# Laying out the bias tables behind the fourth residual tile

## The chip, the cores and the metric

The kernel runs on one core of a Trainium2 chip. The metric is the device time of one execution in microseconds (us), as the median of several runs. One execution was also profiled; every trace number comes from it.

The names of the profile: PE is the matrix engine (PEld its weight loads), DVE the vector engine, ACT the scalar engine, POOL the general engine, SP the engine that here does nothing but issue DMA transfers. All engines run their own instruction streams in order and wait for each other through semaphores.

## The reference

Two layers over 1024 latent tokens of width 1024 and 256 context tokens. Layer zero is grouped attention (16 query heads, 4 key heads, rotary positions), layer one is neighbourhood attention with a learned relative-position bias. Cut to what matters:

```python
for i in range(2):
    hx = rms_norm(x, norm_g[i]) * (1 + sc_x) + sh_x          # adaLN; the same for ctx
    hc = rms_norm(ctx, norm_g[i]) * (1 + sc_c) + sh_c
    if i == 0:
        yx, yc = gqa_axial_mixer(hx, hc, ...)                # (softmax attention * silu(z)) @ a_w_out
    else:
        yx, yc = neighbourhood_mixer(hx, hc, ..., b_rpb)     # scores + bias from b_rpb (16 x 15 x 31)
    x = x + g_x * yx
    if i == 0:
        ctx = ctx + g_c * yc
return rms_norm(x, final_norm_g)
```

In the second layer a query at row r and column c sees 8 rows by 16 columns of keys, and its score gets `rpb[head, dr, dc]`.

The change's title counts from one: "layer one's output projection" is that of the first of the two, called layer zero here.

## The kernel before

Tokens are tiled by 128: eight tiles of x (0 to 7) and two of the context (8 and 9). Weights and activations are split into a high and a low float16 part, and each product is three matmuls. The stages in order of time:

- 0 to about 95 us: modulation columns, the norm of x, keys and values of layer zero. Here the keys are normalised, rotated and split (helper `norm_rope_split`, lines 735 to 762), and their high half is copied to the upper partitions by a DMA (`k<-k`, L831).
- to about 690 us: layer zero's attention, head pair by head pair (`a_proj`, `a_att`, `q_att`). For each pair the row maxima are gathered (`rows`): one DMA transposes them (`zt<-zmax`, L1002), and further DMAs lay the rows into the query tile (`q<-zt`, L1006 and L1008); the score matmuls `st` (L1183, L1184) read that tile. Halves of a last row of heads are taken from `oa` and `oar`, and their outputs for the context from `oc`.
- about 627 to 766 us: layer zero's output projection (`a_out`, matmuls `poa`, L1275). For each token tile t the residual rows are loaded into a tile `x1{t}` (L1262; the trace calls it `x<-in_x`), the gated projection is added, and the sum is written to `x1_d` in DRAM (L1282, `x_d<-x`). The `x1` tiles share one ring of four buffers, so x10 to x13 are loaded first and x14 follows when x10 is free. x13 is the fourth residual tile. The tiles live in a pool that opens when the query projection's pool is closed.
- to about 790 us: the norm of layer one's input (`b_ln`, with DMA transposes `hb_hi<-h16b` and `hb_lo<-l16b`, L661), then its projections (`pb`, `pvz`).
- to the end: layer one's attention (`b_att`), its output projection (`pob`) and the final norm.

The bias of layer one is laid out in DRAM in two steps, both of DMAs from DRAM to DRAM on SP's queue. Sixteen transfers (L1318) copy, for each of 16 grid rows, runs of 16 floats from the input `rpb` into `toe`. Eight transfers (L1321) copy strips of 384 floats from `toe` into `tabd`. Later sixteen loads (L1332) bring one head's table each to SBUF (`tb<-tabd`), where POOL adds the masks (L1333 to L1335) and DVE adds the table to the scores (L1444).

The order of the work on every engine is not the order in which the program writes it. A class `Planner` takes all instructions, builds their dependencies (`graph`), simulates them with a cost of its own for each, and on each engine always starts, of the instructions that are ready, the one with the smallest key; an engine does not stay idle while one is ready, except that SP holds back while its counted DMA work is more than 2 us ahead (`AHEAD`). In the first pass the key is the place in the program; in five more passes it is, for all engines but PE, a due time found by going back from the planned PE order (`deadlines`), and for PE the start in the pass before. The order with the shortest planned time is kept (`refine`) and tied to the instructions (`apply`). So one added tie can move instructions on all engines.

`BEHIND` is a list of pairs (late, early) of tile names. For each pair `graph` finds the DMA copy that writes the late tile and makes it a successor of the DMA copy that writes the early one. The tie is a soft one: the late transfer may start once the early one has been issued, and need not wait for it to land.

Of the kernel before, what the change touches and what calls it, by code (L numbers as in the profile page):

```python
# [40 lines left out]
PFB, PHB, PTB = 5, 5, 8  # L41


BEHIND = [(f"xstage{t}", "wskv7") for t in range(4, 8)]


class Planner:
# [114 lines left out]
    def graph(self):  # L162
# [14 lines left out]
        for x in self.ins:  # L177
# [9 lines left out]
            i = len(self.node)  # L187
# [43 lines left out]
        writer = {}  # L231
        for i, x in enumerate(self.node):
            if type(x).__name__ == "InstDMACopy" and x.outs and hasattr(x.outs[0], "bass_ap"):
                writer.setdefault(x.outs[0].bass_ap.tensor.name.rsplit("_", 1)[0], i)
        for late, early in BEHIND:
            self.soft.add((writer[early], writer[late]))
            self.pred[writer[late]].add(writer[early])

        self.glued = set()
        first = last = None  # L240
# [1418 lines left out]
```

## Time and profile before

| | |
|---|---|
| median of 3 runs | 1366.02 us (1362.78 to 1366.33) |
| the profiled execution's own time | 1365.58 us |
| its span, first to last instruction | 1363.8 us |
| granted PE clock over the span | 0.999 |
| PE, DVE, ACT, POOL busy | 98%, 74%, 67%, 49% |
| toe issues (16) | 47.5 to 65.1 us |
| tabd issues (8) | 68.0 to 77.9 us |
| x1 loads for x10 to x13 | 634.3 to 638.1 us |
| first table load to SBUF | 784.3 us |

The page of the profile gives busy times of the engines over the span, queues, the chain of work that ended last, and groups of instructions by line. Lines such as "PE st L1184 <- DMA q<-zt" say that PE's instruction of line 1184, writing tile st, waited for a DMA that writes q from zt. The engine name SPq means SP's instruction queue, which issues DMAs. A stage's row gives the stretch, its length, and the busy time of each engine in it with the number of instructions in brackets.

### The profile page before, as it was taken

The numbers are of one execution on the slowest core, as the hardware profiler recorded it, in microseconds if no ns is written. First come the engines' busy times: TensorE is split into PE (matmuls) and PEld (weight loads), VectorE is DVE, ScalarE is ACT, GpSimd is POOL, SyncE is SP. The second block draws the span as 40 slices with busy tenths as digits, with TensorE's granted clock in tenths as the row PEclk, the third lists the DMA queues.
The fourth block names the chain that finished last, engine by engine and source line by source line (L and its number), as shares of the span: only waits on it lengthen the run. The fifth ranks groups of instructions, "written<-read, shape, count | busy, mean of one in ns | idle before, by whom it ended". The sixth has DMA issues, their size and how long they took to land.

```text
span 1363.8 us, 34709 instructions
## 1 busy us (share of the span) xinstructions
PE 1329.9 (98%) x13183; PEld 927.6 (68%) x13183; DVE 1003.1 (74%) x2647; ACT 910.2 (67%) x2186; POOL 664.7 (49%) x855
## 2 busy tenths in 40 slices
PE   9999999999999999999999999999999999999897
PEld 6457777777777777776554486777768686867543
DVE  5788788878788789887276846777776867777743
ACT  3653788888787876878632437777776777786711
POOL 2573787777778775788743201312222222332332
PEclk9999999999999999999999999999999999999999
DMA  9652577878789777847066725666576656677932
GB/s 352 186 162 76 108 145 156 154 161 166 149 152 169 146 150 138 172 145 210 10 171 175 178 80 120 125 132 138 117 153 110 156 96 146 113 159 141 194 101 102
DMA packets 426959, 198.23 MB, mean 145 GB/s; under 512 B 382560, under 2 KB 389664, under 8 KB 426792
## 3 DMA queue, kind: packets, MB, share of 16 engines
q1 hardware_dynamic: 426216, 195.98, 65.3%
q8 instruction: 103, 1.69, 0.5%
q14 instruction: 64, 0.52, 0.1%
q10 hardware_dynamic: 576, 0.03, 0.0%
HBM read 90.51 MB, written 15.22 MB: 78 GB/s over the span
## 4 chain that ended last, share of the span: by engine, by line
PE 68%; DVE 11%; ACT 9%; DMA 5%; POOL 3%; issue 3%; SPq 1%; DVEq 0%; POOLq 0%; ACTq 0%
PE pa L946 11%; PE pb L1360 9%; PE pvz L1393 9%; PE poa L1275 7%; PE pob L1566 6%; PE st L1183 2%; PE st L1184 2%; PE pkv L817 2%; ACT bpf L1464 2%; PE pm L976 2%; PE bpv L1473 1%; PE pv L1052 1%; PE qpv L1104 1%; PE pv L1053 1%; PE pv L1051 1%
## 5 line engine op out<-in xcount | busy, mean ns | idle before, releaser
L1045 POOL TENSOR_TENSOR pl<-pf,ph 128x256 f16<-128x256 f32 x340 | 234.1, 714 | 58.2 <-ACT pf L1170 44.5
L1045 POOL TENSOR_TENSOR bph<-bpf,bph 128x256 f16<-128x256 f32 (+1 forms) x128 | 99.9, 790 | 319.5 <-ACT bpf L1464 256.3
L946 PE MATMUL pa<-wa,x 128*128 128x256 f16 x1536 | 213.4, 272 | 0.1
L1360 PE MATMUL pb<-hb_hi,wb 128*128 128x512 f16 (+1 forms) x640 | 193.3, 358 | 1.4 <-DVE bk L1379 1.0
L1393 PE MATMUL pvz<-wb,hb_hi 128*128 128x256 f16 x1024 | 175.4, 273 | 0.6 <-DVE bk L1379 0.3
L946 PEld LDWEIGHTS <-x 128*128 128x128 f16 x1536 | 143.2, 97 | 35.7 <-issue 1.3
L1168 ACT ACTIVATE ph<-st 128x512 f16<-128x512 f32 x200 | 119.1, 604 | 60.7 <-PE st L1184 50.0
L1360 PEld LDWEIGHTS <-wb 128*128 128x128 f16 x960 | 92.7, 98 | 72.5 <-issue 2.9
L1393 PE MATMUL pvz<-wb,hb_lo 128*128 128x256 f16 x512 | 139.6, 273 | 0.0
L1170 ACT ACTIVATE pf<-st 128x512 f32<-128x512 f32 x200 | 119.3, 609 | 1.7 <-POOL pl L1045 1.6
L977 DVE TENSOR_REDUCE mxp<-pm 128x1 f32<-128x512 f32 x160 | 107.9, 684 | 13.7 <-PE pm L976 12.3
L1045 POOL TENSOR_TENSOR qpp<-qpf,qpp 128x512 f16<-128x512 f32 x84 | 97.9, 1186 | 38.4 <-ACT qpf L1127 32.2
L1360 PE MATMUL pb<-hb_lo,wb 128*128 128x512 f16 (+1 forms) x320 | 114.4, 358 | 0.0
L1393 PEld LDWEIGHTS <-hb_hi 128*128 128x128 f16 x1024 | 97.1, 98 | 24.2 <-DVE bk L1379 1.1
L1051 PE MATMUL pv<-v,ph 128*128 128x65 f16 x800 | 104.0, 193 | 0.2 <-ACT ph L1168 0.2
L1052 PE MATMUL pv<-v,ph 128*128 128x64 f16 x800 | 104.0, 195 | 0.0
L1053 PE MATMUL pv<-v,pl 128*128 128x65 f16 x800 | 101.4, 192 | 0.5 <-POOL pl L1045 0.5
L1566 PE MATMUL pob<-wob,ob 128*128 128x512 f16 x384 | 86.7, 379 | 2.6 <-DVE bmx L1444 0.9
L1051 PEld LDWEIGHTS <-ph 128*128 128x128 f16 x800 | 75.8, 97 | 19.0 <-ACT ph L1168 0.7
L1462 ACT ACTIVATE bph<-bpf,bnx 128x384 f16<-128x384 f32 (+1 forms) x128 | 68.7, 582 | 27.2 <-DVE bnx L1454 27.1
L1052 PEld LDWEIGHTS <-ph 128*128 128x128 f16 x800 | 75.5, 97 | 12.6
L1053 PEld LDWEIGHTS <-pl 128*128 128x128 f16 x800 | 76.1, 99 | 10.5 <-POOL pl L1045 1.6
(272 smaller groups left out, 3812.1 us busy)
## 6 DMA issues: line engine op xcount, KB each, us to landing
wg<-in_w_mod SPq DMA_DIRECT2D x64, 256.0 KB
wsb<-in_b_in SPq DMA_DIRECT2D x64, 256.0 KB
wm<-in_w_mod SPq DMA_DIRECT2D x16, 512.0 KB
wsa<-in_a_qz SPq DMA_DIRECT2D x32, 256.0 KB
xstage<-in_x SPq DMA_DIRECT2D x8, 512.0 KB
wsoa<-in_a_w_out SPq DMA_DIRECT2D x16, 256.0 KB
x<-in_x SPq DMA_DIRECT2D x8, 512.0 KB
x_d<-x SPq DMA_DIRECT2D x8, 512.0 KB
```

The source lines that it names most:

```text
L946: T.matmul(ps[:, :, i, :], hA(a, kt, t), wt[w][:, kt, :], start=n == 0, stop=n == 3 * KT - 1)
L977: V.tensor_reduce(mxs[i][:, t, ch:ch + 1], pm, axis=AX.X, op=ALU.max)
L1045: G.tensor_tensor(lo[:, c], p32[:, c], hi[:, c], op=ALU.subtract)
L1051: T.matmul(pv[:, t, :], hi[:, c], v[:, 0:65], start=first and t == 0, stop=False)
L1052: T.matmul(pv[:, t, 0:HD], hi[:, c], v[:, 65:129], start=False, stop=False)
L1053: T.matmul(pv[:, t, :], lo[:, c], v[:, 0:65], start=False, stop=last and t == n - 1)
L1168: S.activation(ph, st, AF.Exp)
L1170: S.activation(p32, st, AF.Exp)
L1275: T.matmul(ps, lhs(a, kt), w[b][:, kt, :], start=n == 0, stop=n == 3 * KT - 1)
L1360: T.matmul(ps[:, 0:n].rearrange("p (t q) -> p t q", q=P), wt[a][:, kt, which * P:(which + 1) * P], hb[b][:, c0 // P:(c0 + n) // P, kt], st ...
L1393: T.matmul(ps[:, :, j, :], hb[a][:, t, kt], wt[w][:, kt, 256:512], start=m == 0, stop=m == 3 * KT - 1)
L1566: T.matmul(ps, ob[kt][:, t // 4, a, c], wout["b"][hf][b][:, kt, :], start=n == 0, stop=n == 3 * KT - 1)
```

## The change

Two pairs join the list: all DMA copies that write `toe` and all that write `tabd` become successors of the load of `x13`. Since these two tensors have 16 and 8 writers, the lookup now keeps a list of writers for each name; the late side takes all of them, the early side the first. The four pairs that were there before have one writer for each name and keep their meaning.

```diff
-BEHIND = [(f"xstage{t}", "wskv7") for t in range(4, 8)]
+BEHIND = [(f"xstage{t}", "wskv7") for t in range(4, 8)] + [("toe", "x13"), ("tabd", "x13")]
...
-                writer.setdefault(x.outs[0].bass_ap.tensor.name.rsplit("_", 1)[0], i)
+                writer.setdefault(x.outs[0].bass_ap.tensor.name.rsplit("_", 1)[0], []).append(i)
         for late, early in BEHIND:
-            self.soft.add((writer[early], writer[late]))
-            self.pred[writer[late]].add(writer[early])
+            for i in writer[late]:
+                self.soft.add((writer[early][0], i))
+                self.pred[i].add(writer[early][0])
```

No transfer is added, dropped or resized, and each `tabd` transfer still waits for the `toe` transfers that it reads.

## The prediction, before the result was known

> **What bounds the kernel now.** I read the page first, then the busy times by stage, then the moved transfers themselves, and last the order of the SP queue and the chain of work around their new place.
>
> ```profile
> span 1363.8 us, 34709 instructions
> PE 1329.9 (98%) x13183; PEld 927.6 (68%) x13183; DVE 1003.1 (74%) x2647; ACT 910.2 (67%) x2186; POOL 664.7 (49%) x855
> ```
>
> PE is busy for 98% of the span, so only what fills or opens a hole in PE can move the end; there are 1363.8 - 1329.9 = 33.9 us of holes. The busy times by stage say where they are (columns: the stretch in us, its length, then the busy time of each engine with its instructions, the granted clock, the DMA engines' busy share, GB/s):
>
> ```profile
> 47.00:80.00 33.00, 29.29 (x159) 14.73 (x157) 30.05 (x62) 24.34 (x54) 30.29 (x42) 1.00 0.62 157
> 80.00:113.00 33.00, 33.00 (x257) 24.27 (x256) 23.92 (x57) 15.18 (x36) 19.40 (x30) 1.00 0.38 109
> 113.00:600.00 487.00, 478.78 (x6006) 365.86 (x6005) 408.02 (x1138) 380.55 (x786) 355.31 (x447) 1.00 0.75 149
> 600.00:648.00 48.00, 47.02 (x622) 31.17 (x621) 39.93 (x80) 37.62 (x76) 37.91 (x51) 1.00 0.64 170
> 648.00:658.00 10.00, 6.72 (x76) 4.05 (x75) 2.74 (x6) 6.64 (x13) 5.85 (x10) 1.00 0.06 20
> 658.00:690.00 32.00, 32.00 (x350) 18.97 (x349) 9.12 (x19) 18.15 (x34) 24.86 (x34) 1.00 0.01 2
> 690.00:790.00 100.00, 100.00 (x479) 46.65 (x478) 77.05 (x118) 37.05 (x66) 33.73 (x31) 1.00 0.76 197
> 790.00:1280.00 490.00, 481.55 (x4461) 356.81 (x4461) 350.57 (x1037) 353.26 (x1039) 123.47 (x172) 1.00 0.64 128
> 1280.00:1364.00 84.00, 75.88 (x418) 36.60 (x415) 34.64 (x74) 19.39 (x57) 25.98 (x26) 0.98 0.42 116
> ```
>
> Two of these stages are the old and the new place of the moved transfers. The old one is 47 to 80 us, as the issues show:
>
> ```profile
> L1318 SPq DMA_DIRECT2D toe<-in_rpb x16: 490/622/1172, 47.5 to 65.1; - x16
> L1321 SPq DMA_DIRECT2D tabd<-toe x8: 599/617/1198, 68.0 to 77.9; - x8
> ```
>
> There PE has a hole of 33.00 - 29.29 = 3.7 us, but DVE is busy for 30.05 and POOL for 30.29 of the 33 us. PE's waits from 30 to 100 us name them:
>
> ```profile
> PE pkv L817 <- DVE t2k L748: 1.3, 1, 1.3
> PE pl L807 <- ACT tf L809: 0.9, 2, 0.6
> PE pkv L817 <- DVE x L813: 0.9, 2, 0.7
> PE pkv L817 <- POOL x L812: 0.5, 1, 0.5
> PE pkv L817 <- DVE wkv L671: 0.2, 1, 0.2
> ```
>
> No DMA is among these 3.8 us. The early stage is bound by the rotation and splitting of the keys, not by the transfers that leave it.
>
> **The change part by part.** It removes nothing. It ties 16 toe and 8 tabd transfers behind the issue (not the landing) of x13, and since the order of all five engines is computed from these ties, the whole order is computed anew.
>
> First, what the transfers cost. Their sizes:
>
> ```profile
> tabd<-toe SPq DMA_DIRECT2D x8, 384.0 KB
> ...
> toe<-in_rpb SPq DMA_DIRECT2D x16, 31.0 KB
> ```
>
> and their run in the old place, SP's issues and then the DMA share:
>
> ```profile
> 47.49 9.79 SPq L1318 DMA_DIRECT2D toe<-in_rpb  x12
> ```
>
> ```profile
> 50.00:60.00 10.00, 7.60 (x39) 3.67 (x37) 9.21 (x23) 8.36 (x20) 8.31 (x12) 1.00 0.43 45
> 60.00:62.00 2.00, 1.48 (x12) 0.69 (x11) 1.71 (x5) 1.47 (x4) 2.00 (x4) 1.00 0.00 0
> ...
> 68.00:80.00 12.00, 11.23 (x63) 5.60 (x62) 10.99 (x20) 7.08 (x16) 11.97 (x17) 1.00 0.87 272
> ```
>
> On SP a toe in a burst takes 9.79 / 12 = 0.82 us, so 16 take 13.1 us; 8 tabd at 0.62 take 5.0. On the DMA engines 10 us at share 0.43 are 4.3 us, for the about 10 toes issued after 49 us: 0.43 us each, 6.9 for all. Tabd: 12 us at 0.87 are 10.4 us, an upper bound, since other transfers share that stretch. Toe to tabd, the wait from the last toe (65.1) to the first tabd (68.0) is 2.9 us.
>
> Leaving the old place: the gain lies between 0 (no wait of PE names a DMA) and 3.7 us (the whole hole). I take 0.3, near zero, since that is what the five waits say. It could be below zero only through the new order, which comes as its own term.
>
> Arriving at the new place. SP's queue there, with x13 the second of the two loads in the first row (the four x1 tiles share one ring and are loaded in order):
>
> ```profile
> 635.95 2.12 SPq L1262 DMA_DIRECT2D x<-in_x  x2
> 639.79 1.13 SPq L1002 DMA_TRANSPOSE zt<-zmax  x1
> 641.01 1.20 SPq L1062 DMA_TRANSPOSE oc<-ol6c  x1
> 642.31 1.00 SPq L1343 DMA_DIRECT2D wsb<-in_b_in  x2
> 643.37 0.57 SPq L629 DMA_DIRECT2D gate_d<-mrow  x1
> 647.34 1.35 SPq L1008 DMA_DIRECT2D q<-zt  x2
> 648.74 0.51 SPq L629 DMA_DIRECT2D gate_d<-mrow  x1
> 689.97 0.33 SPq L1282 DMA_DIRECT2D x_d<-x  x1
> ```
>
> From 649.25 to 689.97 SP issues nothing for 40.7 us, and the stage row says the DMA engines are at 0.01 from 658 to 690. All moved work laid end to end is 13.1 + 2.9 + the larger of 5.0 (issue) and 10.4 (engines) = 26.4 us. It ends at about 676, 14 us before SP's next issue and long before the first reader:
>
> ```profile
> L1332 SPq DMA_DIRECT2D tb<-tabd x16: 326/421/706, 784.3 to 1234.3; - x16
> ```
>
> So the bulk costs nothing; the idle SP and DMA of 649 to 690 cover it. Were that cover gone, it would stand in 690 to 790, where the share is 0.76 (a rival below).
>
> What isn't covered are the toes that the planner puts between x13 and the last q<-zt. The planner never lets SP idle while something is ready, unless its own count of DMA work runs over 2 us ahead, and the toes are ready from x13's issue. All 24 are on SP's queue; no other engine issues them, and POOL's sums from the bias tables come long after. Behind SP there stand zt and q<-zt, the row maxima of the last head pair, for which PE waits:
>
> ```profile
> 639.79 7.53 DMA zt<-zmax
> 647.34 3.37 DMA q<-zt
> ```
>
> ```profile
> 650.75 0.59 PE L1184 MATMUL st<-q,k 65*128 65x512 f16 x2 [2.46 <-DMA q<-zt]
> ```
>
> Their landings are already slow: the pair before it had 610.61 - 608.37 = 2.2 us where this one has 7.5, because the x and wsb loads stand ahead of it on the same rings:
>
> ```profile
> 608.37 1.14 SPq L1002 DMA_TRANSPOSE zt<-zmax  x1
> 610.61 0.72 SPq L1008 DMA_DIRECT2D q<-zt  x1
> ```
>
> SP has gaps: 639.79 - 638.07 = 1.7 us before zt (room for two toes) and 647.34 - 643.94 = 3.4 us before q<-zt (room for four). Toes in these gaps delay no issue, but they stand on the rings ahead of q<-zt: if I put two and one there, 3 x 0.43 = 1.3 us later landing. The ends: 0 (all toes after 649, or the two rows' work absorbed by the slack), and +8.0 with all 16 between the oc transpose and q<-zt (642.21 + 13.1 + 1.6 for wsb and gate_d = 656.9, less the 1.6 that may follow instead, is 655.3 against 647.34). I take +1.2, near the low end, because the urgent zt is ready 1.7 us after x13 and has the earlier due time.
>
> The new order: PE's holes outside the two places are 8.2 us (113 to 600), 8.5 (790 to 1280) and 8.1 (after 1280). A reshuffle can win some of these and lose as much. My estimate is a sixth of the 24.8 us, 4 us either way, and 0 as its middle, since none of these stages touches toe or tabd.
>
> Sum: 1365.58 (the profiled execution) - 0.3 + 1.2 + 0 = 1366.5. That execution stands 0.4 us under the median of the three runs, 1366.02, so this is the median within the noise. A difference under 0.3%, 4.1 us, is about what a measurement of this kernel can't tell from no change.
>
> One rule speaks against the change. In the trace twelve toes of 31 KB were issued from 47.49 on and the DMA engines stood idle by 60, so a toe holds them for at most 12.5 / 12 = 1.04 us. The Trainium skill's page "DMA: Bandwidth & Descriptors", section "Bandwidth", gives about 10.5 ns a packet as the floor of small transfers; with 64-byte runs a toe is 496 packets, which makes 5.2 us, an estimate from that page. By the rule the three toes ahead of q<-zt would add 15.6 us instead of 1.3, and the sum would be 1380.8. The trace doesn't agree: the twelve would have taken 62 us there.
>
> **The rivals.**
>
> Faster through the new order (chance 0.26). Before, the planner didn't foresee zt's slow landing, and PE stood 10.00 - 6.72 = 3.3 us idle from 648 to 658, although output projection matmuls were left to do. With the toes priced in ahead of q<-zt, it may place more of those there; 3.3 us, with some of the 3.7 of the early hole, gives 1365.6 - 5 = about 1360.6. Against it: the early hole names other engines, and the planner doesn't know the queue of x loads any better than before.
>
> Slower, toes ahead of the row maxima (chance 0.18). This is one mechanism with one price: each toe beyond the two that fit before zt, or the four before q<-zt, costs 0.82 us of SP while PE waits in order at st L1184. It decides (over 4.1 us) from five beyond those that fit. With 12 between them it costs 8 x 0.82 = 6.6 us: 1372. If they all go ahead of zt instead, zt is issued at 638.07 + 13.1 = 651.2 and lands in 2.2 us, at 653.4 against 647.34: 1371.6. For it: the non-idling planner. Against it: due times, and the projection matmuls, which the planner can place there if it sees the delay.
>
> Slower, toes late (chance 0.06). If the planner holds toe or tabd beyond 690, 17.3 us of engine time meet a stretch with 24 us free, and the transposes of layer two's input land late. PE has no hole there, so half of tabd, 5 us, is my estimate: 1371.
>
> Slower, toe packets dearer here (chance 0.04). Beside the x loads a toe may take the 1.04 us that the trace allows at most; four ahead of q<-zt cost 4.2 us: 1369.8. The rule of "DMA: Bandwidth & Descriptors" in the Trainium skill would make this case the worst one.
>
> That the change does nothing isn't among them: toes and x13 share SP's queue, so they must move; that it changes no time is my forecast.
>
> **How the numbers follow.** Hidden, within 4.1 us of 1366: 0.46. Faster by more: 0.26. Slower by more: 0.18 + 0.06 + 0.04 = 0.28. The predicted time is that of the likeliest, 1366.5, whose own range is 1362 to 1370. To leave out no more than 2 in 10 the range reaches past the faster case's 1360.6 and the slower case's 1372, each by some of the 4 us of the order: 1357.5 to 1374.
>
> **What would show it.** The toes should start just after x13's issue, most of them behind the last q<-zt, with tabd ended before the first write of x1_d, and the DMA share of 650 to 680 up from about 0 to about 0.5. The stretch from 47 to 80 should keep DVE and POOL at some 30 of 33 us and PE's hole near 3.7. The wait of st on q<-zt should grow from 2.46 us by about 1. I'd be wrong if that wait passes 6 us, if the early hole shrinks by over 2 us, if tabd runs past 690, or if PE's holes from 113 to 600 or after 790 shift by more than 4 us.

## The result and the profile after

The changed kernel takes 1371.08 us, the median of 15 runs (1367.65 to 1375.93), beside 1364.08 us for 15 runs of the kernel before (1360.77 to 1368.72). The ratio is 1.0049, with a 95% interval of 1.0037 to 1.0061: slower by 6.7 us. The forecast was 1366.5 us and no measurable change. The time lies above the 1362 to 1370 given for that likeliest case, and inside the whole range.

The profiled execution of the changed kernel took 1368.75 us and so stands low among its runs; against the 1365.58 of before it shows 3.2 of the 6.7 us. Lines from 238 on are one higher than before. Its page:

```profile
span 1367.0 us, 34716 instructions
...
PE 1330.4 (97%) x13183; PEld 928.0 (68%) x13183; DVE 996.1 (73%) x2647; ACT 911.1 (67%) x2186; POOL 670.6 (49%) x855
```

Its busy times by stage, with the columns as before:

```profile
47.00:80.00 33.00, 29.08 (x156) 14.61 (x154) 30.54 (x69) 23.19 (x52) 30.05 (x40) 1.00 0.17 50
80.00:113.00 33.00, 31.83 (x240) 22.44 (x240) 22.25 (x50) 15.09 (x36) 22.67 (x33) 1.00 0.35 104
113.00:600.00 487.00, 476.57 (x5968) 365.28 (x5967) 400.90 (x1130) 377.59 (x781) 352.14 (x442) 1.00 0.75 148
600.00:648.00 48.00, 45.69 (x604) 30.78 (x601) 42.49 (x90) 37.82 (x76) 35.04 (x48) 1.00 0.57 157
648.00:658.00 10.00, 9.39 (x114) 5.68 (x111) 1.86 (x4) 8.46 (x17) 9.44 (x15) 1.00 0.62 133
658.00:690.00 32.00, 32.00 (x364) 19.21 (x362) 8.49 (x15) 19.98 (x38) 25.93 (x36) 1.00 0.42 107
690.00:790.00 100.00, 100.00 (x489) 46.05 (x488) 75.62 (x119) 35.62 (x63) 37.71 (x30) 1.00 0.73 187
790.00:1280.00 490.00, 481.73 (x4472) 357.50 (x4469) 349.31 (x1029) 352.75 (x1034) 122.96 (x172) 1.00 0.64 129
1280.00:1367.00 87.00, 78.53 (x430) 37.98 (x430) 37.79 (x87) 22.61 (x67) 26.79 (x27) 0.98 0.44 120
```

PE's holes moved like this, each as length less busy time: 47 to 80 us from 3.7 to 3.9, 80 to 113 from 0 to 1.2, 113 to 600 from 8.2 to 10.4, 600 to 648 from 1.0 to 2.3, and 648 to 658 from 3.3 to 0.6. So the stage into which the transfers were moved lost most of its hole. The stages ahead of it gained: next to nothing in the old place itself, and 1.2, 2.2 and 1.3 us in three stages that held none of these transfers before. All holes together grew from 33.9 to 36.6 us, 2.7 of the 3.2 us by which this execution is longer; the rest of the 6.7 us lies in executions that were not profiled. SP's queue at the new place:

```profile
642.56 1.12 SPq L1003 DMA_TRANSPOSE zt<-zmax  x1
643.77 2.07 SPq L1344 DMA_DIRECT2D wsb<-in_b_in  x4
646.67 0.58 SPq L1319 DMA_DIRECT2D toe<-in_rpb  x1
648.92 1.39 SPq L1009 DMA_DIRECT2D q<-zt  x2
650.35 12.09 SPq L1319 DMA_DIRECT2D toe<-in_rpb  x15
662.53 1.14 SPq L630 DMA_DIRECT2D gate_d<-mrow  x2
664.64 5.40 SPq L1322 DMA_DIRECT2D tabd<-toe  x8
692.77 0.34 SPq L1283 DMA_DIRECT2D x_d<-x  x1
```

One toe stands in the gap before q<-zt, fifteen behind it, and the last tabd is issued at 670, 23 us before the next transfer. The DMA engines' share from 650 to 670 us is 0.54, where they had been idle:

```profile
650.00:670.00 20.00, 19.39 (x236) 11.80 (x235) 5.92 (x9) 15.31 (x30) 18.27 (x26) 1.00 0.54 104
```

Most of this is as forecast. One toe stands ahead of q<-zt where three were assumed, and PE has no wait on q<-zt there at all. The added holes lie ahead of the transfers' new place.

### The profile page after: what moved, and what is told of

Its sections match the earlier page's. It is cut to its first block, busy times and chain, and to the rows that moved or that the text cites. A ratio compares the mean times of both kernels' runs of the same rounds, so it can differ in the third digit from the quotient of the medians.

```text
span 1367.0 us, 34716 instructions
## 1 busy us (share of the span) xinstructions
PE 1330.4 (97%) x13183; PEld 928.0 (68%) x13183; DVE 996.1 (73%) x2647; ACT 911.1 (67%) x2186; POOL 670.6 (49%) x855
## 4 chain that ended last, share of the span: by engine, by line
PE 72%; DVE 10%; ACT 7%; DMA 5%; issue 2%; POOL 2%; SPq 1%; DVEq 0%; POOLq 0%; ACTq 0%
PE pa L947 13%; PE pvz L1394 9%; PE pb L1361 9%; PE poa L1276 6%; PE pob L1567 6%; PE st L1184 3%; PE st L1185 3%; PE pm L977 2%; PE bpv L1474 2%; PE pv L1053 2%; PE pv L1054 2%; PE qpv L1105 2%; PE pv L1052 2%; PE qs L1117 2%; PE qs L1118 1%
## 5 line engine op out<-in xcount | busy, mean ns | idle before, releaser
L1046 POOL TENSOR_TENSOR qpp<-qpf,qpp 128x512 f16<-128x512 f32 x84 | 96.8, 1173 | 33.9 <-ACT qpf L1128 31.5
L1054 PEld LDWEIGHTS <-pl 128*128 128x128 f16 x800 | 76.3, 99 | 8.6 <-issue 0.6
```

The source lines that it names most:

```text
L1046: G.tensor_tensor(lo[:, c], p32[:, c], hi[:, c], op=ALU.subtract)
L1054: T.matmul(pv[:, t, :], lo[:, c], v[:, 0:65], start=False, stop=last and t == n - 1)
```

## The experiments

In the experiments the planner runs twice, once without the new ties (A, the order of before) and once with them (B, the order of the changed kernel). Both number the same instructions, so orders can be mixed. `regraft(X, Y, moved)` is order X with the instructions `moved` put behind the neighbours that they have in Y. `splice(X, Y, inside)` gives each engine first those instructions for which `inside` holds, in the order of X, and then the rest in that of Y. `moved` are the 24 transfers. Helper code shifts the line numbers by some 40. Two theories stood at the start: O, the loss is in the new order of the other work; P, the transfers cost at their new place.

**The place alone.** Every engine keeps the order of before; only SP's 24 transfers move.

```diff
-        plan.apply()
+        A.order = regraft(A.order, B.order, moved)
+        A.apply()
```

> PE, DVE, ACT and POOL keep the order of before, instruction for instruction; on SP alone the 24 toe and tabd transfers stand where the changed kernel has them. Theory O (the loss of 0.49% is in the new order of the other work): no loss here, ratio 0.999 to 1.001, and the hole of PE from 648 to 658 us stays near 3.3 us, as the order that filled it is missing. Rival P (the transfers cost at their new place, by SP's time or the rings): ratio 1.004 to 1.006, with a wait of st on q<-zt that grows from 2.5 to over 6 us.

Measured: ratio 1.0009 (0.9998 to 1.0019). The first and last projection matmul of the x tiles before, in the changed kernel, and here, and then PE's wait on q<-zt here between 645 and 660 us:

```profile
L946 PE MATMUL pa<-wa,x x1536: 269/272/282, 94.9 to 602.0; 128*128 128x256 f16 x192
```

```profile
L947 PE MATMUL pa<-wa,x x1536: 269/272/273, 97.1 to 606.8; 128*128 128x256 f16 x192
```

```profile
L987 PE MATMUL pa<-wa,x x1536: 269/272/282, 94.9 to 603.0; 128*128 128x256 f16 x192
```

```profile
PE st L1225 <- DMA q<-zt: 2.0, 1, 2.0
```

Projection starts at 94.9 us as before, and the wait is 2.0 us where it was 2.46 without the toes on the queue. (The hole from 648 to 658 us is 2.5 and not 3.3, but this profile ran part of that stretch at a lower clock, so that the same work filled more of it.) P falls: its ratio of 1.004 lies outside the interval, and the wait that it names did not grow.

**The order alone.** All engines follow the changed kernel, with the transfers back behind their old neighbours.

```diff
-        plan.apply()
+        B.order = regraft(B.order, A.order, moved)
+        B.apply()
```

> All engines have the order of the changed kernel, but the 24 transfers stand behind the same SP neighbours as in the kernel before, at about 47 to 80 us. Theory O: the loss stays, ratio 1.004 to 1.006, first projection matmul pa at about 97 us and not 94.9. Rival P: the loss goes, ratio 0.999 to 1.001.

Measured: ratio 1.0055 (1.0043 to 1.0067), the full loss, with no transfer moved in time. The same row:

```profile
L987 PE MATMUL pa<-wa,x x1536: 269/272/275, 97.5 to 608.6; 128*128 128x256 f16 x192
```

The first projection matmul is 2.6 us late, the last one 6.6 us (608.6 against 602.0); 0.7 us of each is a later start of the first matmul pkv (19.2 against 18.5 us). O holds.

**Where in the order.** Three kernels, transfers at the new place, begin in A's order and go on in B's from planned 100 us, from planned 350 us, and from the planned load of x10 (some 13 us ahead of the hole at 648 to 658). One does the reverse of the first.

```diff
+        own = regraft(A.order, B.order, moved)
+        # e3_early_before; e9_before_to_350 has 350e3, e7_tail_after the start of x10
+        A.order = splice(own, B.order, lambda i: A.start[i] < 100e3 and i not in moved)
+        # e4_early_after
+        A.order = splice(B.order, own, lambda i: B.start[i] < 100e3)
```

> Transfers at the new place; up to planned 100 us (keys and values, start of the first projection) the order of before, from there that of the changed kernel. Theory O with the loss in the key stage: pa starts at 94.9 again and the ratio falls to 1.001 to 1.003 (2.2 of the 7 us are won back). If the loss lies in the attention stage instead: ratio stays 1.004 to 1.005.

> Transfers at the new place; up to planned 100 us the order of the changed kernel, from there that of before. Theory O with the loss in the key stage: pa starts at 97 and the ratio is about 1.002 (2.2 us of 1364 are 1.0016). If the key stage is no cause, ratio 0.999 to 1.001.

> Transfers at the new place; the order of before up to planned 350 us, from there that of the changed kernel. If the attention stage's loss is spread evenly over 100 to 600 us: ratio about 1.002 to 1.003, between e1_place_alone (1.0009) and e3_early_before (1.0041). If it lies in the first half: 1.000 to 1.0015. In the second half: 1.0035 to 1.0045.

> Transfers at the new place; the order of before up to the planned load of x10, from there that of the changed kernel. If the changed order's tail is the better one (its hole from 648 to 658 us is 0.6 and not 3.3 us): ratio 0.998 to 1.000, hole under 1.5 us. If that hole closed only because the work came there 2 to 4 us later: hole 2.5 us or more, ratio 1.000 to 1.002.

| A's order until | ratio | 95% interval |
|---|---|---|
| never (the changed kernel) | 1.0049 | 1.0037 to 1.0061 |
| 100 us (e3_early_before) | 1.0041 | 1.0027 to 1.0054 |
| 350 us (e9_before_to_350) | 1.0024 | 1.0010 to 1.0039 |
| x10 (e7_tail_after) | 1.0004 | 0.9990 to 1.0017 |
| 100 us in B's, then A's (e4_early_after) | 1.0028 | 1.0015 to 1.0041 |

The loss is in no single stage. The ladder's steps are 0.0008, 0.0017 and 0.0020; the intervals of neighbours overlap, so no single step is certain, while its two ends are clear of each other. From the other side the key stage alone costs 1.0028 - 1.0009 = 0.0019, and the same stage is the ladder's 0.0008: the runs don't size it more closely than that. First and last projection matmul, of e3_early_before and then of e4_early_after:

```profile
L987 PE MATMUL pa<-wa,x x1536: 269/272/274, 95.0 to 605.5; 128*128 128x256 f16 x192
```

```profile
L987 PE MATMUL pa<-wa,x x1536: 269/272/282, 96.7 to 605.4; 128*128 128x256 f16 x192
```

With A's first 100 us the projection starts at 95.0, with B's at 96.7. Counted from the first matmul pkv of the same profile, it starts after 76.3 to 76.6 us in the six profiles that have A's order there, and after 78.2 to 78.4 us in the three that have B's (the changed kernel, e2_order_alone, e4_early_after). So the key stage is 1.9 us longer in B's order. The last projection matmul is 3.5 and 3.4 us later here than in the kernel before, against 4.8 in the changed kernel; this figure is less sure, since in the four profiles with A's order up to there it lies anywhere from 581.0 to 584.7 us after the first pkv.

The holes of the second half of the attention show the ladder's last step best. The same stretch, 350 to 600 us, in five kernels, A's order there in the first three (before, e1_place_alone, e7_tail_after):

```profile
350.00:600.00 250.00, 246.62 (x3162) 187.44 (x3160) 210.14 (x580) 196.62 (x406) 184.95 (x235) 1.00 0.79 158
```

```profile
350.00:600.00 250.00, 247.12 (x3166) 187.82 (x3163) 209.58 (x580) 196.84 (x407) 185.04 (x235) 1.00 0.78 158
```

```profile
350.00:600.00 250.00, 246.82 (x3169) 187.77 (x3166) 209.25 (x578) 196.52 (x406) 184.85 (x235) 1.00 0.78 158
```

and B's in the changed kernel and e9_before_to_350:

```profile
350.00:600.00 250.00, 244.83 (x3146) 187.37 (x3144) 205.51 (x572) 196.20 (x405) 183.51 (x233) 0.99 0.79 159
```

```profile
350.00:600.00 250.00, 243.79 (x3132) 185.87 (x3130) 206.00 (x573) 194.81 (x402) 182.88 (x232) 1.00 0.79 158
```

A's order leaves holes of 3.4, 2.9 and 3.2 us, B's 5.2 and 6.2. The other kernels agree: with A's order there, 3.4, 2.2 and 2.5 us in e4_early_after, e11_held_rest_before and e10_tail_old_place; with B's, 6.2, 5.3 and 6.7 in e2_order_alone, e3_early_before and e5_weights_held. From 113 to 350 us there is no such difference (4.3 to 6.5 us in A's order, 4.9 to 6.4 in B's), so the ladder's middle step is not to be seen in the holes. What PE waits for, longest first, from 350 to 648 us, before:

```profile
PE qs L1116 <- DVE mxp L977: 0.9, 2, 0.5
PE st L1183 <- ACT pf L1170: 0.8, 3, 0.4
```

in the changed kernel, and in e9_before_to_350:

```profile
PE st L1184 <- ACT pf L1171: 2.2, 3, 1.2
PE qpv L1105 <- DMA qpt<-qpp: 2.2, 2, 1.8
PE st L1185 <- DMA q<-zt: 2.1, 2, 1.5
```

```profile
PE st L1224 <- ACT pf L1211: 2.0, 3, 1.0
PE pm L1017 <- DVE qmx L1160: 2.0, 2, 1.1
PE qpv L1145 <- DMA qpt<-qpp: 1.7, 2, 1.2
```

Before, no line passes 0.9 us. In B's order PE comes to three kinds of work up to 1.8 us too early: the transposed weights of the attention (qpt, a DMA), the row maxima (zt), and scores that wait for an exponential or a maximum. It reads as if B's order set PE's instructions closer to their producers than these deliver; which swaps did it was not tried.

That e7_tail_after keeps a hole of 2.99 us from 648 to 658 says that the tail of B's order alone need not close it. Why it closed in the changed kernel stays open (see e10_tail_old_place).

**The key stage: a theory that accounts for a part at most.** In this stage B's order differs first where the toes are gone from SP's queue: the next head pair's weights load 8 to 10 us earlier, and are converted on ACT and DVE while these still work on the keys. Busy times from 80 to 90 us of the instructions on those weights alone (PE, DVE, ACT), before and then after:

```profile
80.00:90.00 10.00, 0.00 (x0) 0.01 (x1) 0.00 (x0) 1.00 0.17 48
```

```profile
80.00:90.00 10.00, 0.00 (x0) 1.72 (x3) 1.90 (x3) 1.00 0.32 93
```

Theory W made that the cause. A third plan C has one more tie, which holds the weights back; up to planned 100 us its order is used, then B's or, in the second kernel, A's.

```diff
+HOLD = [("wsa12", "k1", 6)]            # behind the seventh copy k<-k
+        C.order = splice(C.order, B.order, lambda i: C.start[i] < 100e3)     # e5_weights_held
+        C.order = splice(C.order, own, lambda i: C.start[i] < 100e3)         # e11_held_rest_before
```

> The changed kernel, but up to planned 100 us the order comes from a plan with one more tie: the load wsa12 of the next head pair's weights (and with it wsa13, which shares its ring) waits for the seventh copy k<-k, so that its conversions on ACT and DVE leave the key stage, as in the kernel before. From planned 100 us the changed kernel's order. Theory W (with the transfers gone from SP's queue the next weights were loaded and converted 8 to 10 us earlier, in the stage that DVE and POOL bound): pa starts at 95.0 to 95.8 and not 97, the ratio falls to 1.0035 to 1.0045, near that of e3_early_before (1.0041). Rival N (the delay comes from POOL's and DVE's other reordering between 60 and 75 us): pa stays at 96.5 to 97.5, ratio 1.005 to 1.0055.

> As e4_early_after (1.0028: early order of the changed kernel, then that of before), but with the load wsa12 held back to the seventh copy k<-k in the early order. Theory W (earlier weight conversions make the key stage's loss): pa starts 0.8 to 1.5 us earlier than in e4's order and the ratio falls to 1.001 to 1.002, toward e1_place_alone (1.0009). Rival N (the other reordering of that stage): ratio 1.0025 to 1.0035.

Measured: 1.0056 (1.0039 to 1.0073) and 1.0027 (1.0018 to 1.0037). The same weights' row in e11_held_rest_before, and PE's longest waits for POOL from 30 to 113 us in e4_early_after and in it:

```profile
80.00:90.00 10.00, 0.00 (x0) 1.49 (x3) 0.63 (x1) 1.00 0.15 39
```

```profile
PE pkv L858 <- POOL x L853: 1.5, 2, 1.0
...
PE pkt L868 <- POOL q16k L803: 1.3, 1, 1.3
```

```profile
PE pkv L859 <- POOL x L854: 1.5, 2, 1.0
...
PE pkv L859 <- POOL xc_hi L854: 0.2, 1, 0.2
```

Of ACT's 1.90 us in the stretch 0.63 are left, DVE still has 1.49 of 1.72, and PE's wait for the split keys (q16k, 1.3 us) is gone. The projection starts at 96.5 us against 96.7, and at 96.3 in e5_weights_held. Counted from the first pkv, these are 77.6 and 77.7 us against 78.4 and 78.2 without the hold: 0.8 and 0.5 of the stage's 1.9 us. The times don't show it (1.0027 against 1.0028, 1.0056 against 1.0049). So W is not the whole price. It may be a part of it, and as most of DVE's conversions stayed where they were, its size is not settled. The wait for the cast of x on POOL, 1.5 us in both and 0.5 before, stays, which fits the rival of a reordered POOL queue; it wasn't tried by itself.

**Other places and one mix.** The mix that might have beaten both kernels, A's order to x10 and then B's, with the transfers at their old place:

```diff
+        A.order = splice(A.order, B.order, lambda i: A.start[i] < A.start[A.writer["x10"][0]])
```

> Transfers back at 47 to 80 us; the order of before up to the planned load of x10, from there that of the changed kernel. This is the one mix that could beat both: if the changed order's tail were better, ratio 0.997 to 0.999; e7_tail_after (1.0004, with the transfers late) speaks for 0.999 to 1.001, which would also say that the place of the transfers is worth under 0.1% either way.

Measured: 1.0004 (0.9992 to 1.0016), exactly as with the transfers late. Its row of 648 to 658 us:

```profile
648.00:658.00 10.00, 9.39 (x119) 5.83 (x117) 3.91 (x7) 8.84 (x19) 7.88 (x12) 1.00 0.01 3
```

The hole is 0.6 us here, and the time is no better for it. Nor did the work come later: the last projection matmul starts at 600.5 us. The hole follows PE's wait on q<-zt, 0.7 us here and 2.4 in e7_tail_after with the same order but for the 24 transfers. That wait does not follow the transfers' place either: with the transfers late it is 2.0, 2.4 and 2.4 us in e1_place_alone, e7_tail_after and e11_held_rest_before, and 0.6 in e4_early_after; with the transfers early it is 2.5 in the kernel before.

Two kernels change one name each, and the planner orders everything anew:

```diff
-... [("toe", "x13"), ("tabd", "x13")]
+... [("toe", "wsa40"), ("tabd", "wsa40")]     # e8_tie_mid
+... [("toe", "x14"), ("tabd", "x14")]         # e12_tie_x14
```

> One word differs from the changed kernel: the transfers are tied to the load wsa40 (about 340 us) instead of x13, and the planner orders everything anew. Theory W: they are gone from the key stage all the same, so pa starts at about 97 and the ratio is at least 1.0015. The rest is another order: if the loss of the attention stage is a property of any plan without the transfers early, ratio 1.004 to 1.006; if it is one order's luck, the ratio may be anything from 1.001 to 1.006, and PE's hole from 113 to 600 us differs from 10.4 us by over 1 us.

> The changed kernel with x14 in place of x13: nearly the same order of all engines, but the transfers now stand among the transposes of layer one's input, from about 705 us on. By the rival of late transfers they would cost some 5 us there: ratio 1.008 to 1.009. If PE, without a hole from 690 to 790, hides them: ratio 1.004 to 1.006 as the changed kernel.

e8_tie_mid: 1.0102 (1.0085 to 1.0119), above every figure that was expected. Its stretch from 113 to 350 us:

```profile
113.00:350.00 237.00, 227.49 (x2738) 174.40 (x2736) 190.67 (x546) 177.12 (x368) 160.98 (x202) 0.99 0.74 147
```

A hole of 9.5 us, where the kernel before has 4.8 (232.16 of 237 busy) and the changed one 5.3. The expectation erred on the place too: the toes ran from 207 to 253 us, amid the attention, so place and order aren't separated in this kernel. It shows how far one name can move the time, not why. A part goes with the clock: its six runs have a mean clock of 0.9950, beside 0.9981 in the runs of the kernel before that were taken with them; by an estimate, 0.0031 x 1364 = 4 of its 14 us.

e12_tie_x14: 1.0059 (1.0044 to 1.0073). Its toes, and the stretch from 690 to 790 us:

```profile
L1319 SPq DMA_DIRECT2D toe<-in_rpb x16: 490/622/823, 707.7 to 737.3; - x16
```

```profile
690.00:790.00 100.00, 99.05 (x483) 45.35 (x482) 78.86 (x118) 35.29 (x64) 35.72 (x30) 1.00 0.91 225
```

The DMA share rises from the changed kernel's 0.73 to 0.91, PE's hole from 0 to 0.95 us, and the ratio can't be told from 1.0049. The 5 us that the prediction gave to late transfers don't show; since the whole order is computed anew here too, their price alone is not measured.

## Where the prediction was right, and where it was wrong

**The number.** The time lies inside the whole range by luck. The likeliest case ended at 1370, and the bound of 1374 was set by the rival of toes ahead of the row maxima (1372), which did not happen: one toe went ahead. The base of the sum, 1365.58, was also high; 15 runs of the kernel before give 1364.08. So the sum forecast 0.9 us of loss, and 6.7 us were measured.

**What bounds the kernel.** Right for the old place: no transfer fills or opens a hole there. With the order held, the early projection starts at 94.9 us whether the toes are there or not. The 0.3 us of gain can't be seen. That only holes of PE count is not quite so: PE's own work is stretched where the clock falls after a wait (last section).

**The cost of the moved work.** Right in size. An end at about 676 us was forecast; the last tabd was issued at 670.0, and the DMA engines were busy to about 676.5 (a share of 0.94 from 674 to 676 and 0.22 from 676 to 678). Their shares of 0.54 and 0.33 from 650 to 670 and 670 to 690 make 17.4 us of engine time, where 17.3 were forecast. It was hidden in SP's idle stretch. One toe went ahead of q<-zt where three were assumed. At the 5.2 us that the prediction's dearest estimate gives a toe, 16 of them would have taken 83 us.

**The toes ahead of the row maxima.** The +1.2 us agree with the 0.0009 of e1_place_alone (0.0009 x 1364 = 1.2 us, interval -0.3 to 2.6), but that is luck: the wait on q<-zt, which was to make them, didn't grow. Nor did the toe ahead of q<-zt hold it up by a time that can be seen: from zt's issue to that of q<-zt it took 7.6 us before, 7.8 in e1_place_alone and 6.4 in the changed kernel with one toe between, and 7.8 in e10_tail_old_place with none. Two other pairs differ in the place alone: the changed kernel (1.0049) and e2_order_alone (1.0055), e7_tail_after and e10_tail_old_place (1.0004 both). Together they give the place no measurable price. The slower rivals assumed places that the planner didn't choose (a dozen toes ahead, or transfers beyond 690 us), so they explain none of the loss; their prices as such were not measured.

**The new order.** This is the step that failed. "0 as its middle, since none of these stages touches toe or tabd" took the order term for noise of 4 us either way. It measured 0.0049 - 0.0009 = 0.0040, 5.5 us, by the changed kernel, and 0.0055, 7.5 us, by e2_order_alone. The reason given was not a reason: the planner reorders stages that don't touch the tied transfers, so there was no ground for zero as the middle. Nor was it so: the loads tb<-tabd run from 784.3 to 1234.3 us, through the stage from 790 to 1280. None of the new orders that were run was measurably faster than before.

**The faster rival.** Its hole closed, as described (3.3 to 0.6 us), and no time came of it: e10_tail_old_place closes the same hole to 0.6 us, without the losses ahead of it, and measures 1.0004.

**The sign to look for.** "PE's holes from 113 to 600 or after 790 shift by more than 4 us" was too coarse a test. The loss showed as 0.2, 1.2, 2.2 and 1.3 us in four stages, and less 2.7 in the fifth. "The wait of st on q<-zt should grow from 2.46 us by about 1" failed: the changed kernel has no such wait there.

Not settled: which swapped instructions open the attention's holes, what makes up the key stage's 1.9 us, where the part of the loss lies that the profiled execution doesn't show, and whether another order under the same ties would have been faster than before.

## What to carry to other kernels

Where a planner sets the order, a tie is an edit of every engine's queue; price the moved work and the new order as two terms, and test them as two kernels, one with the old order and the work moved, one with the new order and the work left. For the order term the holes of stages that the edit doesn't name are the evidence, and several small ones can add up to the whole change. A hole that closes is no gain by itself: here it closed twice, and neither time was shorter.

## What the runs showed of the hardware

In the profiled execution of e1_place_alone the granted clock fell shortly after the wait of 2.0 us in PE's hole from 648 to 658 us, which ended at 651.2 (columns as in the stage rows; the third from the end is the clock):

```profile
654.00:658.00 4.00, 4.00 (x34) 2.83 (x33) 1.13 (x2) 3.10 (x6) 3.43 (x6) 0.50 0.54 48
```

It was 0.50 for these 4 us, and 1.00 throughout the same hole in the kernel before (0.999 over its span). The attention's holes can bring the same: in the changed kernel PE waits 1.85 us for qpt, until 554.4 us, and then the clock falls too:

```profile
556.00:558.00 2.00, 2.00 (x15) 0.96 (x13) 1.98 (x6) 0.71 (x3) 2.00 (x3) 0.50 0.00 0
```

At 466 to 472 us, after waits of 1.1 and 0.8 us, e2_order_alone and e5_weights_held show such a dip as well, and no profile with A's order shows one between 113 and 648 us. From 554 to 560 us the clock was 0.82, 0.50 and 0.83 in turn, which by an estimate costs 2 x (0.18 + 0.50 + 0.17) = 1.7 us of PE's work besides the hole. Over the changed kernel's 15 runs the mean clock is 0.9971 (0.995 to 0.999), beside 0.9981 in 20 runs of the kernel before that were taken with e1_place_alone. An estimate from this is 0.0010 x 1367 = 1.4 us, so lower clocks may be a fifth of the loss of 6.7 us. What sets a dip off was not tried. The Trainium skill, "TensorE: Matmul & The Clock Gate", section "Part 1: The HAM clock gate", has the clock drop to half after an idle window of about 3.4 us: the 0.50 agrees with the half, but the same hole ended with a drop after waits of 2.0 and 2.4 us (e1_place_alone, e7_tail_after) and without one after 2.46 and 2.4 us (before, e11_held_rest_before), so when it drops is not read from the hole's length here.

One start-up differs by 1 us with the same instructions: the first matmul pkv came at 18.5 us in the kernel before and at 19.6 in e7_tail_after, whose order is the same there. A start time of one profile can thus be off by about 1 us, less than the differences of 1.7 to 2.6 us that are read above.
